# The start of a two-layer decoder trunk: x loaded over two queues ahead of everything else, matmuls of ones first, and the first norm taken from a second copy of x

## The chip, the cores and the metric

One core of one Trainium2 chip runs the whole program. The metric is device microseconds of one execution; the lower the better. The program's times below are the median of three executions, and the profile is of one more execution.

## What is computed

The reference is a trunk of two layers (DEPTH = 2) on 512 tokens of width 1024, all in float32. Only the start of a layer matters here:

```python
for i in range(DEPTH):
    h = rmsnorm(x, norm_g[i])
    z = h @ w_in[i]
    (a_q, a_k, ..., i_q, i_k, i_w, ..., merge) = jnp.split(z, offsets, axis=-1)
    ...
def rmsnorm(x, g):
    xf = x.astype(jnp.float32)
    y = xf * lax.rsqrt(jnp.mean(xf * xf, axis=-1, keepdims=True) + EPS)
    return (y * g.astype(jnp.float32)).astype(x.dtype)
```

After the projection each layer runs three attention mixers, three gated up-projections, an output projection and a gated per-layer embedding. A last rmsnorm gives the output. Rotary angles come from `positions`: cos and sin of position times eight frequencies.

## The kernel before

**Layout.** The residual x lies transposed, features on partitions: eight tiles `X` of 128 features by 512 tokens (KT = 8). A projection gives 128 output features by 512 tokens in one PSUM bank. The row factor of the norm (one over the root mean square of a token) is not applied to x but to the products afterwards, so products can start before it is known. The gain `norm_g` is applied to x at once, from the first eight columns (`ng`) of a table of small parameters called `small` (505 columns).

**Three matmuls for one.** Every operand is split into a high part, rounded to the fp32r format that TensorE takes in one pass, and the remainder: `HI` and `LO` for x (`scaled_split`, ACT and DVE), `whi` and `wlo` for weights (`weights`, ACT or POOL for the first, DVE or POOL for the second). A product of 128 features is HI by whi, LO by whi and HI by wlo for each of eight feature tiles: 24 matmuls of 512 columns (`product`). Weights come in pieces of 128 by 512 (`raw`, four buffers) by DMAs that SP issues, two pieces to a product.

**The start of layer 0.** The first unit of weights (`IKBK`) and the eight `X` tiles are loaded on SP. ACT issues the loads of the positions (`posi`), the frequencies (`inv`), `small` and the constants (`consts`: identity and masks). Then come three products of 24 matmuls each (IKBK, IQ0, IQ1) and the token products (`tok_product`): 4 pairs of weight tiles, tokens on the PSUM partitions, 352 columns, 96 matmuls. In between, `statistics` squares the eight `X` tiles on ACT (`square`), adds them up on DVE or POOL, sums over the partitions with 16 one-column matmuls against `ones` (`rms_stats`; each is float32 and runs as two instructions, so eight calls), forms the factor with an integer guess and three Newton steps of small DVE instructions (`rsqrt`), and spreads it over a tile `R` with one float32 matmul. `angles` makes cos and sin: some 20 DVE instructions on 128 by 32 elements in a row, each reading the one before, with the two Sin activations on ACT at the end. `rope_tables` transposes cos and sin on TensorE and multiplies them by `R`; every product of queries and keys needs the result.

**What sets the order.** Nothing is issued as written. Each call is recorded in a `Plan`; `Plan.put_down` (L387) then walks a list schedule: an operation has a cost per engine (`Plan.cost`, L336) and a rank, its place in the program plus `plan.shift`; each engine takes what could start first, with a small price for a late rank. The result is a fixed order of instructions on each engine, written out at L468, which is why all rows of the profile carry that line. Engines then run in this order, each waiting for its inputs. A DMA is issued by an engine's own instruction stream (SP's or ACT's), in its place in that order.

**Completion counters of DMAs.** Under the plan, the tile framework gives each DMA one of eight completion counters in turn (`DMAHW0` to `DMAHW7`). A DMA that takes a counter waits, at its issue, until the DMA that had this counter before it has landed, whichever queue that one is on. In the built program this stands as a wait on the issuing instruction.

Of the kernel before, what the change touches and what calls it, by code (L numbers as in the profile page):

```python
# [15 lines left out]
AF = mybir.ActivationFunctionType  # L16
ALU = mybir.AluOpType
# [4 lines left out]
EPS = 1e-6  # L22
# [10 lines left out]
NWS = 4  # L33
NKB = 10
URGE = 0.002
THETA = 500000.0

SPLITS = (
# [180 lines left out]
class Plan:  # L219
# [116 lines left out]
    def cost(self, engine, op):  # L336

        if op.call == "dma_start":
            return 0.65, 2.4
        n = max(x.columns() for x in op.ins + op.outs)  # L340
        psum = any(x.tile.space == "psum" for x in op.ins + op.outs)
        if engine == "tensor":
# [44 lines left out]
    def put_down(self):  # L387
        names = ("tensor", "vector", "scalar", "gpsimd", "sync")
        free = dict.fromkeys(names, 0.0)
        port = 0.0  # L390
        held = {(e, o.seq): self.shares(e, o) for o in self.ops for e in o.engines}

        def begin(e, op):
# [30 lines left out]
        while done < len(self.ops):  # L424
            best = None
            for e in names:
                pick = None
                for op in can[e]:
                    at = begin(e, op)
                    key = at + (0.0 if e == "tensor" else URGE) * op.rank  # L430
                    if pick is not None and (pick[2], pick[1].rank) < (key, op.rank):
                        continue
                    if len(op.engines) > 1 and e != min(op.engines, key=lambda x: finish(x, op)):
                        continue
                    pick = (at, op, key)
                if pick and (best is None or pick[0] < best[0]):
                    best = (pick[0], e, pick[1])
            if best is None:
                raise RuntimeError("the plan is stuck")
            at, e, op = best  # L440
            us, lag = (op.us, op.lag) if e == op.engines[0] else self.cost(e, op)
            op.engine, op.start = e, at
            free[e] = at + us
            if held[e, op.seq]:
                port = at + us
            for x in op.engines:
                can[x].remove(op)
            done += 1
            end = at + us + lag
            for o in op.next:  # L450
                o.ready = max(o.ready, at + us if o.engines == (e,) and op.call != "dma_start" else end)
                o.left -= 1
                enter(o)
            for t in op.tiles.values():
                t.uses -= 1
                t.end = max(t.end, end)
                if t.uses == 0 and t.space != "dram":
                    slots[t.ring].append((t.end, t.slot))
                    give(t.ring)
# [9 lines left out]


@with_exitstack
def trunk_kernel(ctx, tc, xT, pT, pos, freq, W, WK, small, con, out):
    nc = tc.nc
    plan = Plan(tc)
    V, G, A, T, SY = [plan.engine(e) for e in ("vector", "gpsimd", "scalar", "tensor", "sync")]
# [44 lines left out]
        return t.bitcast(F32)  # L520

    posi = const("posi", [P, NQ], I32)
    A.dma_start(posi, pos)
    inv = const("inv", [P, 8], F32)
    A.dma_start(inv, freq)
    consts = const("consts", [P, NCO], F32)
    ident = consts[:, CO["ident"][0] : CO["ident"][1]]
    mask = consts[:, CO["mask"][0] : CO["mask"][1]]
# [1 line left out]
    valid = consts[:, CO["valid"][0] : CO["valid"][1]]  # L530
    ones = const("ones", [P, P], F32)
    V.memset(ones, 1.0)


    def rsqrt(y, v, n, off=False):
# [27 lines left out]

    def rms_stats(sums):

        pst = tr_ps()
        for b in range(NQ):
            c = slice(b * P, (b + 1) * P)
            T.matmul(pst[:, b : b + 1], sums["acc"][:, c], ones[:, 0:1], start=True, stop=False)
            T.matmul(pst[:, b : b + 1], sums["last"][:, c], ones[:, 0:1], start=False, stop=True)  # L570
        ms = sb("ms", (P, NQ), bufs=2)
        V.tensor_scalar(ms, pst[:, 0:NQ], 1.0 / D, EPS, ALU.mult, ALU.add)
        rstd = sb("rstd", (P, NQ), bufs=2)
        rsqrt(rstd, ms, NQ)
        prb = tr_ps()
# [10 lines left out]
        SY.dma_start(raw[:, : src.shape[1]], src)  # L586
        return raw

    def weights(src, n):

        his, los = [], []
        step = S // n * n
        for c in range(0, src.shape[1], step):
            w = min(step, src.shape[1] - c)
            raw = load_raw(src[:, c : c + w])
            hi = sb("whi", (P, S), F32R, pool=wp, bufs=NWS)
            lo = sb("wlo", (P, S), F32R, pool=wp, bufs=NWS)
            AG.copy(hi[:, :w], raw[:, :w])
# [10 lines left out]
    sin8 = const("sin8", [P, NQ, 8], F32)  # L609
    cos8 = const("cos8", [P, NQ, 8], F32)  # L610
    nsin8 = const("nsin8", [P, NQ, 8], F32)
    A.activation(sin8[:, 0, 0:1], ones[:, 0:1], AF.Sin)

    def angles():

        V.tensor_copy(posf, posi)
# [40 lines left out]
    sums = {}  # L657
    for l in range(L):
        sm = plan.tile(lp, (P, NSM), F32, nm("small"), "small", 1)
        A.dma_start(sm, small[l])  # L660

        def par(name, a=0, n=None):
            s0, s1 = SM[name]
# [3 lines left out]


        if l == 0:
            have["w"] = weights(W[l, UNIT["IKBK", 0]], P)  # L670
            xs = []
            for d in range(KT):
                t = sb("X", pool=bp)
                SY.dma_start(t, xT[:, d, :])
                xs.append(t)
            A.dma_start(consts, con)
            resid = [xT[:, d, :] for d in range(KT)]
        else:
            resid = []
# [15 lines left out]
            return his, los  # L695

        HI, LO = scaled_split(xs, "ng")
        if l == 0:
            angles()


        def tok_product(pieces, n, evac, banks):
# [13 lines left out]

        def statistics():
            if l == 0:
                for t in xs:
                    square(sums, t)  # L720
            rstd, R, _ = rms_stats(sums)
            if l == 0:
                Cr, Sr = rope_tables(R)
# [657 lines left out]
def _arrange(x, p, positions, norm_g, w_in, diff_lambda, diff_subln_g,  # L1381
# [56 lines left out]
    for i in range(NQ):  # L1438
# [3 lines left out]
        con[:, CO["valid"][0] + i] = (t[:, 0] >= 31).astype(np.float32)  # L1442
    return {
        "xT": np.ascontiguousarray(x[0].T.reshape(KT, P, S).transpose(1, 0, 2)),
        "pT": np.ascontiguousarray(p[:, 0].transpose(0, 2, 1).reshape(L, 2, P, S).transpose(0, 2, 1, 3)),
        "pos": np.ascontiguousarray(positions[0].reshape(NQ, P).T),
        "freq": freq,
# [17 lines left out]
```

## Time and profile before

| | us |
|---|---|
| time, median of 3 (1420.03 to 1420.48) | 1420.24 |
| the profiled execution's own time | 1421.58 |
| its span, first to last instruction | 1419.8 |
| TensorE matmuls busy, share of the span | 1380.1 (97%) |
| DVE, ACT, POOL busy | 1050.4, 784.6, 586.2 |
| mean granted TensorE clock | 0.992 |
| moved by DMA | 115.5 MB read, 4.7 MB written |

The busy time of TensorE says that it has something in flight nearly always; idle stretches are at the start, around 30 to 62 us, and in the last 25 us. The granted clock is given as a share of full speed; 1.00 is 2.4 GHz and 0.50 is 1.2 GHz.

### The profile page before, as it was taken

Reading aid. Unit: us, or ns where it says so; the run is one execution under the profiler, and the core shown is the slowest. Engines: PE = TensorE matmul, PEld = TensorE weight load, DVE = VectorE, ACT = ScalarE, POOL = GpSimd, SP = SyncE. Lnnn points to the kernel's source line nnn. Section 1 sums busy time; section 2 is a strip of 40 time slices with the busy share of each in tenths; the row PEclk is TensorE's granted clock in tenths of the full one; section 3 lists DMA queues with packets and bytes.
Section 4 is the critical chain, followed back from the end, with each engine's and each line's share of the span. In section 5 each row is a group of like instructions: output and inputs, shape, how many; then the busy total and the mean of one; then the engine's idle time right before and its main releaser. Section 6 shows DMA issues by size and latency. Waiting matters only on the chain.

```text
span 1419.8 us, 20706 instructions
## 1 busy us (share of the span) xinstructions
PE 1380.1 (97%) x6842; PEld 1151.0 (81%) x6842; DVE 1050.4 (74%) x2346; ACT 784.6 (55%) x1820; POOL 586.2 (41%) x623
## 2 busy tenths in 40 slices
PE   7899999999999999999999999999999999999995
PEld 5788887888888888888888888878888888888884
DVE  7768888878887566556885888888888855656664
ACT  4556666766764456324444666666676644643431
POOL 3646468544453152121452744873455323313120
PEclk9999999999999999999999999999999999999997
DMA  5222322111222221343422232312112222124321
GB/s 171 92 74 81 105 88 67 60 61 60 68 74 82 83 89 60 107 145 102 142 80 98 82 97 62 95 59 69 60 60 75 67 89 85 61 83 156 94 81 60
DMA packets 67069, 121.56 MB, mean 86 GB/s; under 512 B 7696, under 2 KB 10000, under 8 KB 66960
## 3 DMA queue, kind: packets, MB, share of 16 engines
q1 hardware_dynamic: 61632, 110.91, 24.7%
q10 hardware_dynamic: 5328, 9.31, 1.9%
q8 instruction: 54, 0.88, 0.2%
q14 instruction: 55, 0.45, 0.1%
HBM read 115.48 MB, written 4.72 MB: 85 GB/s over the span
## 4 chain that ended last, share of the span: by engine, by line
PE 87%; POOL 3%; DVE 3%; issue 2%; ACT 1%; DVEq 0%; POOLq 0%; ACTq 0%
PE mm L468 69%; PE at L468 19%; POOL nt L468 1%; DVE t L468 1%; POOL Q L468 1%; POOL t L468 1%; POOL wlo L468 1%; DVE BV L468 0%; ACT t L468 0%; POOL whi L468 0%; ACT o L468 0%; DVE pc L468 0%; DVE wlo L468 0%; POOL K L468 0%; ACT P L468 0%
## 5 line engine op out<-in xcount | busy, mean ns | idle before, releaser
L468 PE MATMUL mm<-HI,whi 128*128 128x512 f32 x1232 | 496.5, 404 | 10.2 <-ACT HI L468 9.3
L468 PE MATMUL mm<-HI,wlo 128*128 128x512 f32 x1232 | 486.1, 395 | 0.3
L468 PE MATMUL mm<-LO,whi 128*128 128x512 f32 x1232 | 484.9, 394 | 0.0
L468 POOL TENSOR_SCALAR whi<-raw 128x512 fp32r<-128x512 f32 (+1 forms) x188 | 128.5, 685 | 530.7 <-PE mm L468 381.5
L468 POOL TENSOR_TENSOR wlo<-raw,whi 128x512 fp32r<-128x512 f32 (+1 forms) x198 | 268.8, 1361 | 176.7 <-ACT whi L468 160.3
L468 PEld LDWEIGHTS mm<-HI,whi 128*128 128x128 f32 x1232 | 232.5, 189 | 49.2 <-ACT HI L468 9.3
L468 PEld LDWEIGHTS mm<-HI,wlo 128*128 128x128 f32 x1232 | 231.7, 188 | 49.9 <-DVE wlo L468 1.1
L468 ACT CAST whi<-raw 128x512 fp32r<-128x512 f32 (+1 forms) x208 | 126.9, 612 | 255.6 <-PE mm L468 194.4
L468 PEld LDWEIGHTS mm<-LO,whi 128*128 128x128 f32 x1232 | 232.5, 189 | 39.3 <-issue 0.7
L468 DVE TENSOR_TENSOR wlo<-raw,whi 128x512 fp32r<-128x512 f32 (+1 forms) x198 | 146.2, 742 | 81.2 <-ACT whi L468 44.5
L468 ACT ACTIVATE P<-P,mx 128x512 f32<-128x512 f32 (+3 forms) x256 | 142.4, 557 | 67.9 <-DVE mx L468 67.2
L468 PE MATMUL at<-K,Q 128*128 128x256 f32 (+3 forms) x608 | 139.0, 325 | 1.4 <-DVE VW L468 1.1
L468 PEld LDWEIGHTS at<-K,Q 128*128 128x128 f32 x608 | 104.1, 189 | 19.3 <-ACT VS L468 1.4
L468 DVE TENSOR_TENSOR t<-mm,R 128x512 f32<-128x512 f32 x100 | 68.9, 689 | 59.5 <-PE mm L468 56.7
L468 DVE CUSTOM_DVE_ANT_0 P<-at,consts 128x128 f32<-128x128 f32 x208 | 93.4, 469 | 20.4 <-PE at L468 19.6
L468 DVE TENSOR_TENSOR PTl<-at,PTh 128x512 fp32r<-128x512 f32 x192 | 87.0, 484 | 26.8 <-ACT PTh L468 20.0
L468 POOL TENSOR_TENSOR Q<-t,Q 64x512 fp32r<-64x512 f32 x64 | 87.1, 1361 | 33.9 <-ACT Q L468 27.1
L468 ACT ACTIVATE P<-P,rc 128x128 f32<-128x128 f32 x192 | 92.1, 552 | 9.5 <-DVE rc L468 8.8
L468 PE MATMUL at<-consts,P 128*128 128x128 f32 x560 | 96.1, 273 | 0.3 <-DVE P L468 0.3
L468 ACT CAST PTh<-at 128x512 fp32r<-128x512 f32 x192 | 74.2, 420 | 36.2 <-PE at L468 32.2
L468 PEld LDWEIGHTS at<-consts,P 128*128 128x128 f32 x560 | 71.8, 140 | 23.0 <-DVE P L468 1.2
L468 PE MATMUL mm<-BRh,whi 128*128 128x512 f32 x192 | 77.0, 406 | 0.0
(209 smaller groups left out, 2146.7 us busy)
## 6 DMA issues: line engine op xcount, KB each, us to landing
raw<-W SPq DMA_DIRECT2D x396, 256.0 KB, 2.6
raw<-WK SPq DMA_DIRECT2D x16, 176.0 KB, 2.2
X<-xT SPq DMA_DIRECT2D x8, 256.0 KB, 6.8
X<-xT ACTq DMA_DIRECT2D x8, 256.0 KB, 3.2
res<-X ACTq DMA_DIRECT2D x8, 256.0 KB, 2.0
X<-res ACTq DMA_DIRECT2D x8, 256.0 KB, 3.2
out<-t SPq DMA_DIRECT2D x6, 256.0 KB, 2.6
K<-pT ACTq DMA_DIRECT2D x4, 256.0 KB, 3.3
```

Source lines behind the costliest of these rows:

```text
L468: getattr(getattr(self.nc, op.engine), call)(*real, **kw)
```

## The change

Five edits. (1) `small` is loaded in two pieces, its first eight columns before all else, the rest later. (2) The eight `X` tiles are issued in turn by ACT (even) and SP (odd), four behind each piece of the first weights; `posi`, `inv`, the rest of `small`, `consts` and the first use of the Sin table come behind them on ACT. (3) Nine float32 matmuls of `ones` by `ones`, 128 by 128 each, stand ahead of the first product and write a spare bank. (4) In layer 0 the sum of squares of a token comes from `xN`, x with tokens on partitions: four loads of 128 by 1024 (512 KB each) on SP, and one Square activation with `accum_out` for each; the eight squares, their additions and the one-column matmuls go, in layer 0 alone. `angles` is called behind these. (5) The planner's cost of a DMA: 0.5 us on the issuing engine instead of 0.65, landing 1.4 us later instead of 2.4, plus 0.1 us and bytes at 370 GB/s on one shared wire.

```diff
@@ Plan.cost
         if op.call == "dma_start":
-            return 0.65, 2.4
+            return 0.5, 1.4
@@ Plan.put_down
+            if op.call == "dma_start":
+                tile = (op.outs + op.ins)[0]
+                end = wire = max(end, wire) + 0.1 + tile.shape[0] * tile.columns() * 4 / 370000.0
@@ trunk_kernel
     posi = const("posi", [P, NQ], I32)
-    A.dma_start(posi, pos)
     inv = const("inv", [P, 8], F32)
-    A.dma_start(inv, freq)
...
     V.memset(ones, 1.0)
+    spare = at_ps()
+    for _ in range(WARM):
+        T.matmul(spare[:, :P], ones, ones, start=True, stop=True)
...
     def rms_stats(sums):
-        pst = tr_ps()
-        for b in range(NQ):
-            c = slice(b * P, (b + 1) * P)
-            T.matmul(pst[:, b : b + 1], sums["acc"][:, c], ones[:, 0:1], start=True, stop=False)
-            T.matmul(pst[:, b : b + 1], sums["last"][:, c], ones[:, 0:1], start=False, stop=True)
+        if "rows" in sums:
+            total = sums["rows"]
+        else:
+            total = tr_ps()[:, 0:NQ]
+            for b in range(NQ):
+                c = slice(b * P, (b + 1) * P)
+                T.matmul(total[:, b : b + 1], sums["acc"][:, c], ones[:, 0:1], start=True, stop=False)
+                T.matmul(total[:, b : b + 1], sums["last"][:, c], ones[:, 0:1], start=False, stop=True)
         ms = sb("ms", (P, NQ), bufs=2)
-        V.tensor_scalar(ms, pst[:, 0:NQ], 1.0 / D, EPS, ALU.mult, ALU.add)
+        V.tensor_scalar(ms, total, 1.0 / D, EPS, ALU.mult, ALU.add)
...
-    def weights(src, n):
+    def weights(src, n, between=()):
...
             raw = load_raw(src[:, c : c + w])
+            for fetch in between[c // step :][:1]:
+                fetch()
...
-    A.activation(sin8[:, 0, 0:1], ones[:, 0:1], AF.Sin)
...
-        A.dma_start(sm, small[l])
+        if l == 0:
+            A.dma_start(sm[:, 0:KT], small[l, :, 0:KT])
+        else:
+            A.dma_start(sm, small[l])
...
         if l == 0:
-            have["w"] = weights(W[l, UNIT["IKBK", 0]], P)
-            xs = []
-            for d in range(KT):
-                t = sb("X", pool=bp)
-                SY.dma_start(t, xT[:, d, :])
-                xs.append(t)
+            xs = [sb("X", pool=bp) for _ in range(KT)]
+
+            def fetch(*tiles):
+                for d in tiles:
+                    (SY if d % 2 else A).dma_start(xs[d], xT[:, d, :])
+
+            have["w"] = weights(W[l, UNIT["IKBK", 0]], P, (lambda: fetch(0, 1, 2, 3), lambda: fetch(4, 5, 6, 7)))
+            A.dma_start(posi, pos)
+            A.dma_start(inv, freq)
+            A.dma_start(sm[:, KT:], small[l, :, KT:])
             A.dma_start(consts, con)
+            A.activation(sin8[:, 0, 0:1], ones[:, 0:1], AF.Sin)
...
-        if l == 0:
-            angles()
...
         def statistics():
             if l == 0:
-                for t in xs:
-                    square(sums, t)
+                sums["rows"] = sb("ss", (P, NQ), bufs=2)
+                for b in range(NQ):
+                    plan.shift = 70 * (b // 2)
+                    t = sb("P", (P, 1280), bufs=3)[:, :D]
+                    SY.dma_start(t, xN[b])
+                    A.activation(t, t, AF.Square, accum_out=sums["rows"][:, b : b + 1])
+                plan.shift = 0
+                angles()
```

**ACT's start.** What stands first on ACT before, with the waits of each instruction (the number behind a name tells buffers apart; DVE, Pool and Activation are the counters of those engines):

```order
L468 DMA posi_77<-pos 128x4
L468 DMA inv_89<-freq 128x8
L468 ACT_TABLE_LOAD
L468 ACTIVATE sin_8_93<-ones_79 128x1 [waits DVE_49]
L468 DMA small_97<-small 128x505
L468 DMA consts_101<-con 128x772 [waits DMAHW0_49]
L468 CAST whi_105<-raw_81 128x512 [waits DMAHW1_49]
L468 CAST whi_111<-raw_91 128x512 [waits DMAHW3_49]
L468 ACTIVATE t_117<-X_95 128x512 [waits DMAHW4_49]
L468 ACTIVATE HI_123<-X_95,small_97 128x512 [waits DMAHW6_49]
```

And on ACT in the changed kernel:

```order
L472 DMA small_79<-small 128x8
L472 DMA X_87<-xT 128x512
L472 DMA X_95<-xT 128x512
L472 DMA X_109<-xT 128x512
L472 DMA X_115<-xT 128x512 [waits DMAHW0_49]
L472 DMA posi_121<-pos 128x4 [waits DMAHW2_49]
L472 DMA inv_125<-freq 128x8 [waits DMAHW4_49]
L472 DMA small_79<-small 128x497 [waits DMAHW5_49]
L472 DMA consts_134<-con 128x772 [waits DMAHW7_49]
L472 ACT_TABLE_LOAD
L472 ACTIVATE sin_9_138<-ones_77 128x1 [waits DVE_49]
L472 ACTIVATE HI_142<-X_87,small_79 128x512
```

Nine DMA issues instead of four now stand ahead of the first `HI`, five of them with a wait for an earlier DMA; the one of `consts` waits for counter 7, which was last taken by `raw_107`.

**SP's start.** SP in the changed kernel (before, it issued raw, raw, the eight X in a row, then four raw):

```order
L472 DMA raw_81<-W 128x512
L472 DMA X_89<-xT 128x512
L472 DMA X_97<-xT 128x512
L472 DMA raw_107<-W 128x512
L472 DMA X_113<-xT 128x512 [waits DMAHW1_49]
L472 DMA X_119<-xT 128x512 [waits DMAHW3_49]
L472 DMA raw_127<-W 128x512 [waits DMAHW6_49]
L472 DMA raw_130<-W 128x512 [waits DMAHW0_49]
L472 DMA P_136<-xN 128x1024 [waits DMAHW1_49]
L472 DMA P_140<-xN 128x1024 [waits DMAHW2_49]
L472 DMA P_144<-xN 128x1024 [waits DMAHW3_49]
L472 DMA raw_152<-W 128x512 [waits DMAHW4_49,DVE_49]
```

`raw_107` is SP's fourth load, and three of the four loads of `xN` now stand ahead of the weights of the third product (`raw_152`).

**TensorE in the third product.** The transposes of cos and sin (`at_301`, `at_329`) stood behind the one-column matmuls and among the token products before; now they stand in the third product (`mm_297`):

```order
L472 MATMUL mm_211<-HI_194,wlo_228 128x512
L472 MATMUL mm_297<-HI_142,whi_290 128x512
L472 MATMUL at_301<-consts_134,t_83 128x128 x4
L472 MATMUL mm_297<-LO_148,whi_290 128x512
L472 MATMUL mm_297<-HI_142,wlo_295 128x512
L472 MATMUL mm_297<-HI_146,whi_290 128x512
L472 MATMUL mm_297<-LO_156,whi_290 128x512
L472 MATMUL mm_297<-HI_146,wlo_295 128x512
L472 MATMUL mm_297<-HI_154,whi_290 128x512
L472 MATMUL at_329<-consts_134,t_91 128x128 x4
```

`t_83` holds cos, which needs all of `angles` before it, and 23 matmuls of the third product stand behind its transposes.

## Rows read from the trace of the kernel before

**Rows 1.** The page, part 1: busy us, share of the span, instructions of TensorE.
```profile
PE 1380.1 (97%) x6842; PEld 1151.0 (81%) x6842; DVE 1050.4 (74%) x2346; ACT 784.6 (55%) x1820; POOL 586.2 (41%) x623
```
**Rows 2.** Waits of TensorE, 0 to 60 us: us in total, times, longest.
```profile
PE mm L468 <- ACT HI L468: 9.3, 1, 9.3
PE mm L468 <- ACT whi L468: 1.5, 1, 1.5
PE mm L468 <- DVE t L468: 1.1, 1, 1.1
```
**Rows 3.** Timeline of TensorE, first product: start us, us, engine, line, operation.
```profile
11.12 0.63 PE L468 MATMUL mm<-HI,whi 128*128 128x512 f32 x1
11.55 0.63 PE L468 MATMUL mm<-LO,whi 128*128 128x512 f32 x1
...
12.73 0.40 PE L468 MATMUL mm<-LO,whi 128*128 128x512 f32 x1
...
12.97 0.40 PE L468 MATMUL mm<-HI,wlo 128*128 128x512 f32 x1
```
**Rows 4.** Timeline of ACT, 0 to 5 us; idle time and releaser in brackets.
```profile
1.64 1.28 ACT L468 ACT_TABLE_LOAD   x1 [1.64 <-PEq L1457]
...
3.62 0.33 ACTq L468 DMA_DIRECT2D consts<-con  x1
4.00 1.14 ACT L468 CAST whi<-raw 128x512 fp32r<-128x512 f32 x2 [0.86 <-DMA posi<-pos]
```
**Rows 5.** SP's third and fourth load: issue in the timeline; KB and us to landing.
```profile
1.63 0.90 SPq L468 DMA_DIRECT2D X<-xT  x2
...
X<-xT SPq DMA_DIRECT2D x2, 256.0 KB, 6.5
```
**Rows 6.** Windows: us, busy (x) per engine, clock, DMA share, GB/s.
```profile
2.00:6.00 4.00, 0.00 (x0) 0.00 (x0) 1.52 (x4) 2.26 (x4) 0.00 (x0) 1.00 0.86 248
6.00:14.00 8.00, 4.69 (x13) 3.45 (x14) 4.88 (x11) 5.41 (x9) 0.00 (x0) 1.00 1.00 373
```
**Rows 7.** Groups by form, 0 to 30 us, ACT, DVE, POOL: xcount, busy us, mean ns.
```profile
L468 ACT ACTIVATE HI<-X,small 128x512 fp32r<-128x512 f32 x8 | 5.3, 718 | 0.6 <-DMA X<-xT 0.6
L468 ACT ACTIVATE t<-X 128x512 f32<-128x512 f32 x8 | 4.5, 620 | 2.9 <-DMA X<-xT 2.9
...
L468 DVE SCALAR_TENSOR_TENSOR LO<-X,small,HI 128x512 fp32r<-128x512 f32 x8 | 5.9, 791 | 3.0 <-ACT HI L468 3.0
...
L468 POOL TENSOR_TENSOR wlo<-raw,whi 128x512 fp32r<-128x512 f32 x3 | 4.2, 1413 | 0.2
L468 POOL TENSOR_TENSOR wlo<-raw,whi 128x352 fp32r<-128x352 f32 x3 | 3.1, 1042 | 2.0 <-ACT whi L468 1.9
```
**Rows 8.** Timeline of DVE and ACT, the chain of `angles`.
```profile
15.55 5.97 DVE L468 SCALAR_TENSOR_TENSOR ang<-kk,ang 128x32 f32<-128x32 f32 x8
...
22.20 0.65 DVE L468 SCALAR_TENSOR_TENSOR ang<-kk,ang 128x32 f32<-128x32 f32 x3
...
24.61 0.23 ACT L468 ACTIVATE cos<-kk 128x32 f32<-128x32 f32 x1 [1.28 <-DVE kk L468]
```
**Rows 9.** Timeline of TensorE at the one-column matmuls and the transposes behind them.
```profile
30.41 0.38 PE L468 MATMUL at<-ones,g 128*128 128x1 f32 x2 [0.59 <-DVE g L468]
...
32.22 0.64 PE L468 MATMUL at<-consts,t 128*128 128x128 f32 x4
```
**Rows 10.** Windows, as rows 6: right behind rows 9, and near the end of the program.
```profile
32.60:36.20 3.60, 3.60 (x17) 3.60 (x16) 3.19 (x20) 0.59 (x1) 0.00 (x0) 0.57 0.39 123
1402.00:1403.00 1.00, 1.00 (x6) 1.00 (x6) 0.00 (x0) 0.00 (x0) 0.00 (x0) 0.50 0.00 0
```
**Rows 11.** Timeline of TensorE at 1401.68 us: idle time in brackets.
```profile
1401.68 0.47 PE L468 MATMUL at<-ones,t 128*128 128x1 f32 x2 [3.78 <-ACT t L468]
```
**Rows 12.** Timeline of ACT and TensorE: `R`, and the first weights behind the token products.
```profile
37.39 0.58 ACT L468 COPY R<-at 128x512 f32<-128x512 f32 x1 [3.91 <-PE at L468]
...
48.55 0.50 PE L468 MATMUL mm<-whi,HI 128*128 128x512 f32 x1 [1.54 <-ACT whi L468]
```

More of the change, by code (lines that the diff above doesn't have):

```diff
@@ L35 @@
 URGE = 0.002
+WARM = 9
 THETA = 500000.0
@@ L389, in put_down @@
         free = dict.fromkeys(names, 0.0)
-        port = 0.0
+        port = wire = 0.0
         held = {(e, o.seq): self.shares(e, o) for o in self.ops for e in o.engines}
@@ L471, in trunk_kernel @@
 @with_exitstack
-def trunk_kernel(ctx, tc, xT, pT, pos, freq, W, WK, small, con, out):
+def trunk_kernel(ctx, tc, xT, xN, pT, pos, freq, W, WK, small, con, out):
     nc = tc.nc
@@ L1444, in _arrange @@
         "xT": np.ascontiguousarray(x[0].T.reshape(KT, P, S).transpose(1, 0, 2)),
+        "xN": np.ascontiguousarray(x[0].reshape(NQ, P, D)),
         "pT": np.ascontiguousarray(p[:, 0].transpose(0, 2, 1).reshape(L, 2, P, S).transpose(0, 2, 1, 3)),
```

## The prediction

> **What bounds the kernel now.** Read the page first: TensorE's matmuls are busy 97% of the span [rows 1], so nearly all of the 1419.8 us is TensorE's own work, which the change leaves alone but for a few instructions. What can be won or lost is time in which TensorE stands still or runs slowly, and the change touches only the first 50 us or so. So read next who TensorE waits for there, then the stretch as a timeline. TensorE's first matmul waits 9.3 us for the first `HI` [rows 2]. The first eight matmuls then start 0.43 us apart, later ones 0.23 to 0.24 [rows 3]: 512 columns at 1.2 and at 2.4 GHz. (The clock column says 1.00 in this stretch [rows 6]; here the spacing is the better witness.) At 30.41 us comes a wait of 0.59 us and then 1.8 us of one-column matmuls, up to the transposes at 32.22 [rows 9]; right behind them the granted clock is 0.57 for 3.6 us [rows 10]. Then there are waits of 1.1 and 1.5 us [rows 2], the last ending at 48.55 us, at the first weights behind the token products [rows 12].
>
> I count what TensorE loses up to that matmul. 9.3 for the start; 8 x 0.2 = 1.6 at half clock; 0.6 + 1.8 = 2.4 for the statistics; (1 - 0.57) x 3.6 = 1.5 for the clock behind them; 1.1 + 1.5 = 2.6. Sum 17.4. Useful until then: 72 matmuls of 512 columns at 0.23, 68 token matmuls at 352/512 of that, 0.16, eight transposes at 0.64/4 = 0.16 [rows 9] and about 1 us for the matmul of `R`: 29.7. As 48.55 - 29.7 = 18.9, another 1.5 goes in waits too small to list.
>
> **When the first product starts.** This decides most. ACT issues nine DMAs ahead of its first `HI`, and the last, `consts`, waits for the landing of `raw_107`, SP's fourth load. That such a wait holds the instructions behind it is shown before: the issue of `consts` at 3.62 us waited for `posi`, and the copy `whi` behind it began only at 4.00, with that DMA as the releaser [rows 4]. SP's third and fourth loads before were issued at 1.63 and 2.1 us and landed 6.5 us later [rows 5]; so I take 8.6 us for `raw_107`, the row that is nearest. Bounds: seven loads of 262 KB share the way; all at the later rate of 373 GB/s from 2 us on gives 6.9 us; at the early 248 GB/s up to 6 us, and in equal shares with what ACT has put behind, 9.5 us [rows 6]. Then on ACT the issue 0.33, the table load 1.28 [rows 4], a short Sin 0.23 [rows 8] and the first `HI` 0.72 [rows 7]: 2.6 us. First matmul at 11.2 us (9.5 to 12.1): 1.9 us later than before, not earlier.
>
> **The matmuls of ones.** Nine, each between 0.16 us (a transpose of 128 columns, one instruction at full clock [rows 9]) and four times that, 0.64 (two instructions at half clock), from about 1 us on: done between 2.5 and 6.8 us. They cost nothing, since TensorE idles until 11.2 anyway; were that cover gone and the first `HI` there at 5 us, they would cost up to 1.8. What they are for is likely lost: in this trace an idle time of 3.78 us [rows 11] was followed by a clock of 0.50 [rows 10], and here at least 4.4 us lie between them and the first product.
>
> **The first product** is paced by DVE: eight `LO` of 0.79 and one `wlo` of about 0.7 make 7.0 us [rows 7] against 24 x 0.23 = 5.5 of matmuls. It loses 1.5; a half clock start hides in this but for some 0.3. I take 1.8 (1.5 to 2.2).
>
> **The transposes in the third product.** TensorE reaches `at_301` after 49 matmuls: 11.2 + 11.3 + 1.8 = 24.3 us. It needs cos in `t_83`. DVE, from 11.2 on: eight `LO` and three `wlo`, 8.4 us, then some 30 instructions of 0.22, since three took 0.65 [rows 8], 6.6 us, and 0.3 for ACT's cos: 26.5 us with DVE undisturbed. But before, eight such instructions took 5.97 us instead of 1.8 [rows 8], while POOL ran `wlo` instructions of 1.41 and 1.04 us [rows 7]. In the changed order three of POOL's (1.4 + 1.0 + 1.0 = 3.4) can fall into this stretch: 29.9 us. Between ends so alike in kind I take half, 28.2: TensorE stands for 3.9 us (2.2 to 5.6). That is about the idle time that ended at half clock [rows 10, 11]; eight slow matmuls would cost 1.6 [rows 3]; I count half, 0.8.
>
> **The statistics.** Gone are the 2.4 us and the 1.5 us of low clock behind them. The four Squares of 1024 columns are about 1.24 us each (twice 0.62 [rows 7]), beside TensorE's work; but the last two stand behind cos on ACT, with a table load, a `whi`, a copy and a DMA issue between: 5.5 us from cos, so 32.9. Behind that on DVE two shuffles and some sixteen short instructions, 5 us: 37.9. TensorE gets to the matmul of `R` at 28.2 + 1.3 + 5.3 + 3.4 + 0.8 = 39.0, so it does not wait for it (0 to 1.5; I take 0.3). `R` is there 2.6 us later than before [rows 12]. The table load for Exp and what DVE waits for from it now lie ahead of `R`, which shortens the way from `R` to 48.55 from 11.2 to about 9.8 us: 49.8. TensorE, with 59 token matmuls in between (9.4 us), is there at 49.4 and waits 0.4.
>
> **The loads of xN.** 2.1 MB more, 5.6 us at 373 GB/s. Queued behind three of them is `raw_152`: 5.6 MB from 2 us on, by the two rates, land by 18.5 us; `whi` and `wlo` 2 us more. TensorE wants them at 24, so 3.5 us of cover hide them; without it each of the three would cost 1.4. The fourth waits for the first Square and is in by 24, ahead of ACT's 31.
>
> **The planner's costs** reorder neighbours in the rest of the program, with the same work on each engine; I count 0, and 1 us to either side.
>
> **Sum.** 11.2 + 1.8 + 3.9 + 0.8 + 0.3 + 0.4 = 18.4 against 18.9: TensorE is 0.5 us ahead in work (12 more token matmuls are done), while the first matmul behind them comes 1.2 us later. What follows hangs on both in turn, so I take the middle, +0.3 us. Against the profiled execution that is 1421.6 + 0.3 = 1421.9; the median of the runs lies 1.3 lower, so **1420.5 us**: no change that could be measured (0.2%, 2.8 us, is about what a measurement of this kernel can tell).
>
> **Rivals.**
>
> *Early release, faster.* `raw_107` lands at 6.9 us and POOL's `wlo` miss the chain of `angles`: first matmul 9.5, stall 2.2, no fall of the clock. 1.7 + 1.7 + 0.8 = 4.2 us better: 1416.3. For it: the small loads `posi` and `inv` no longer stand in the early stretch that ran at 248 GB/s. Against it: in that stretch both queues already had loads outstanding, so a second queue alone is no cure. The Trainium skill, "DMA: Bandwidth & Descriptors", section "Issuing engines are not separate DMA queues", says that loads issued by different engines run on the same sixteen DMA engines and that spreading them saves only the time of issuing; by it x lands no sooner for being on two queues, and the sum stands. Chance 0.24.
>
> *The queue doesn't hold ACT at all*, and the first `HI` follows its own tile, at about 4.6 us: first matmul near 6, another 3.5 us off: 1412.8. Rows 4 speak against it. Chance 0.04.
>
> *A late cos, slower.* `raw_107` at 9.5 and all three of POOL's `wlo` in the way: first matmul 12.1, `t_83` at 30.8, a stall over 5 us and half clock for sure behind it. 0.9 + 1.7 + 0.8 = 3.4 us, 1423.9. It decides from the point where the stall passes 3.8 us. For it: on DVE before, most of this chain was lost to POOL. Chance 0.29.
>
> *The ones hold the clock* through 4.4 idle us or more. Then the start is at full speed, but DVE paces the product: 0.3 us, inside the forecast.
>
> **Numbers.** Forecast, within 0.2%: 0.43, its own range 1417.6 to 1422.9. Faster 0.24 + 0.04 = 0.28, slower 0.29. The range for 8 in 10, with the ends of both rivals and the 1 us of the planner: 1415.5 to 1425.0.
>
> **What would show it.** In the profile after: the first `HI` behind a table load that follows the issue of `consts`, with `raw_107` landing just before; first matmul at 11 us, spaced 0.43; the second stall of TensorE at the transposes of cos, of 2 to 6 us, released by DVE; no one-column matmuls and no clock of 0.5 near 33 us; then a first matmul on later weights near 50 us. The prediction is wrong if the first `HI` starts before 8 us, or if TensorE doesn't stop at the transposes.

## The result, and the profile after

The changed kernel takes **1430.32 us** (median of 4 runs, 1428.42 to 1433.41) against 1420.36 us (4 runs, 1420.03 to 1421.41): a ratio of 1.0072, 95% interval 1.006 to 1.0085. It is 10 us slower. The forecast was 1420.5 us, range 1415.5 to 1425.0, so the time lies outside it. The profiled execution took 1433.41 us, the longest of the four.

The page's first part, against [rows 1]: TensorE, DVE, ACT and POOL have nearly the same work in a span that is 11.8 us longer.

```profile
span 1431.6 us, 20707 instructions
...
PE 1385.0 (97%) x6844; PEld 1153.3 (81%) x6844; DVE 1055.0 (74%) x2347; ACT 781.4 (55%) x1815; POOL 575.9 (40%) x621
```

**The start came out much as forecast.** ACT's timeline, to set against [rows 4]: the issue of `consts` is held until 8.44 us, the table load behind it has `raw` (SP's fourth load) as its releaser, and the first `HI` begins at 10.21 us, although the first X tile had landed at 5.3 us.

```profile
8.44 0.33 ACTq L472 DMA_DIRECT2D consts<-con  x1
8.80 1.28 ACT L472 ACT_TABLE_LOAD   x1 [8.80 <-DMA raw<-W]
10.10 0.20 ACT L472 ACTIVATE sin<-ones 128x1 f32<-128x1 f32 x1
10.21 5.00 ACT L472 ACTIVATE HI<-X,small 128x512 fp32r<-128x512 f32 x8
```

TensorE's timeline, against [rows 3, 9]: first matmul at 11.05 us; the next two follow after 0.70 and 0.59 us, then they start 0.43 us apart until 14.05, at a granted clock of 0.50; a wait of 3.15 us at the transposes of cos and sin, and again 0.43 us behind it; 1.28 us at the matmul of `R`. The windows below it are to be read as [rows 10]: the granted clock is 0.50 behind the wait at 27.19 us, and once more in layer 2. (From here on the two layers are called 1 and 2; layer 1 is what the sections ahead call layer 0.)

```profile
11.05 0.77 PE L472 MATMUL mm<-HI,whi 128*128 128x512 f32 x1 [6.39 <-ACT HI L472]
...
13.62 0.63 PE L472 MATMUL mm<-HI,wlo 128*128 128x512 f32 x1
14.05 0.45 PE L472 MATMUL mm<-HI,whi 128*128 128x512 f32 x1
14.33 0.39 PE L472 MATMUL mm<-LO,whi 128*128 128x512 f32 x1
...
27.19 0.66 PE L472 MATMUL at<-consts,t 128*128 128x128 f32 x4 [3.15 <-DVE t L472]
...
28.43 0.63 PE L472 MATMUL mm<-HI,whi 128*128 128x512 f32 x1
28.86 0.63 PE L472 MATMUL mm<-LO,whi 128*128 128x512 f32 x1
...
39.78 1.13 PE L472 MATMUL at<-t,ones 128*128 128x512 f32 x2 [1.28 <-DVE t L472]
```
```profile
27.80:31.20 3.40, 3.40 (x12) 2.71 (x11) 1.07 (x4) 2.98 (x5) 0.00 (x0) 0.50 0.12 37
939.30:942.50 3.20, 3.20 (x9) 2.43 (x9) 3.10 (x10) 1.76 (x3) 2.76 (x6) 0.50 0.00 1
```

**Most of the loss lies far behind the start**, where no edit touched the computation. Who TensorE waits for between 60 and 1370 us, in the kernel before (us in total, times, longest):

```profile
PE at L468 <- ACT o L468: 3.7, 8, 0.5
PE at L468 <- ACT t L468: 1.1, 1, 1.1
PE mm L468 <- DVE VW L468: 1.0, 1, 1.0
PE mm L468 <- POOL whi L468: 0.9, 2, 0.5
```

and in the changed kernel, where waits for DVE's `t`, `wlo`, `gate` and `hr` are new. Two of these rows still belong to the start: the wait for POOL's `whi` ends at 59.80 us and that for `gate` at 63.87.

```profile
PE at L472 <- ACT o L472: 4.0, 8, 0.6
PE at L472 <- DVE t L472: 3.2, 2, 1.6
PE mm L472 <- DVE wlo L472: 1.6, 2, 1.0
PE at L472 <- POOL whi L472: 1.4, 1, 1.4
...
PE mm L472 <- DVE gate L472: 1.1, 1, 1.1
PE mm L472 <- DVE hr L472: 0.9, 2, 0.4
```

To see where time is lost, each instruction of DVE, ACT and POOL is paired with the one of the same name in the kernel before (counted from the end, since the tail is the same work), and the difference of their starts is taken; its median over 20 us is the **lag**. In us, for the profiled execution of the changed kernel and of six runs that follow:

| at us | changed | e1 | e2 | e10 | e4 | e11 | e12 |
|---|---|---|---|---|---|---|---|
| 100 | 3.1 | 2.2 | -2.3 | 0.7 | -6.8 | -6.6 | -6.5 |
| 180 | 4.1 | 2.3 | -0.4 | 0.9 | -5.0 | -6.5 | -4.0 |
| 300 | 6.8 | 2.3 | 3.3 | 0.9 | -0.8 | -6.4 | -6.6 |
| 760 | 7.4 | 2.8 | 3.5 | 1.4 | -0.1 | -6.0 | -6.2 |
| 1000 | 12.2 | 3.1 | 6.6 | 1.8 | 3.3 | -4.7 | -7.9 |
| 1400 | 12.0 | 2.9 | 5.7 | 1.7 | 3.3 | -5.0 | -8.0 |

The changed kernel's lag grows in two places: 100 to 300 us and 760 to 1000 us, which are the attention mixers of layer 1 and of layer 2. Layer 2 does not use the copy of x, nor the loads or matmuls that were moved. What those two places share is the order in which the plan put their instructions. Compared instruction by instruction, the two programs differ behind 130 us only in what the plan decides: nearly all differences lie between 140 and 400 us and between 820 and 1070 us, on TensorE, DVE, ACT and POOL; the loads on SP stand in the same order.

### The profile page after: what moved, and what is told of

It is laid out like the page before. It is cut to its first block, busy times and chain, and to the rows that moved or that the text cites. A ratio compares the mean times of both kernels' runs of the same rounds, so it can differ in the third digit from the quotient of the medians.

```text
span 1431.6 us, 20707 instructions
## 1 busy us (share of the span) xinstructions
PE 1385.0 (97%) x6844; PEld 1153.3 (81%) x6844; DVE 1055.0 (74%) x2347; ACT 781.4 (55%) x1815; POOL 575.9 (40%) x621
## 4 chain that ended last, share of the span: by engine, by line
PE 88%; DVE 5%; ACT 1%; POOL 1%; issue 0%; DVEq 0%; POOLq 0%; ACTq 0%
PE mm L472 69%; PE at L472 19%; DVE t L472 2%; DVE P L472 0%; POOL nt L472 0%; DVE cm L472 0%; ACT o L472 0%; ACT t L472 0%; DVE g L472 0%; DVE wlo L472 0%; DVE K L472 0%; DVE x L472 0%; DVE hr L472 0%; DVE BV L472 0%; DVE X L472 0%
## 5 line engine op out<-in xcount | busy, mean ns | idle before, releaser
L472 POOL TENSOR_SCALAR whi<-raw 128x512 fp32r<-128x512 f32 (+1 forms) x193 | 131.4, 682 | 550.7 <-PE mm L472 392.5
L472 POOL TENSOR_TENSOR wlo<-raw,whi 128x512 fp32r<-128x512 f32 (+1 forms) x194 | 260.9, 1349 | 175.6 <-ACT whi L472 148.3
L472 ACT CAST whi<-raw 128x512 fp32r<-128x512 f32 (+1 forms) x203 | 123.8, 613 | 260.5 <-PE mm L472 194.6
```

The lines of the kernel that those rows point to most:

```text
L472: getattr(getattr(self.nc, op.engine), call)(*real, **kw)
```

## Experiments

Each time is a median; the ratio is to the kernel before on the same chip, with its 95% interval. Theory A: the planner's new DMA costs (edit 5) reorder the attention parts. Theory B: the late start alone. Theory D: the list schedule's order is arbitrary. A2, named from the second set on, joins A and D: the plan falls into one of a few orders, and the cost of the order adds to that of the start.

### Edit 5 taken back (e1), and alone (e2)

```diff
-            return 0.5, 1.4
+            return 0.65, 2.4
...
-            if op.call == "dma_start":
-                tile = (op.outs + op.ins)[0]
-                end = wire = max(end, wire) + 0.1 + tile.shape[0] * tile.columns() * 4 / 370000.0
```

> The changed kernel with the planner's old DMA costs (0.65 us, landing 2.4 us later, no shared wire); edits 1 to 4 stay. Theory A (the new costs swap neighbours in the attention parts of both layers, and this loses some 7 of the 10 us): 1422 to 1424 us, the first at<-K,Q still near 52.6 us as in the changed kernel (50.3 before), and no further lag behind it. Theory B (the late start alone, everything behind it merely shifted or knocked on): 1429 to 1431 us. Theory D (the order that a list schedule falls into is arbitrary; any small change of costs moves it by several us to either side): any value from 1418 to 1432, not tied to edit 5.

Measured: 1423.55 us, ratio 1.0018 (1.0009 to 1.0027).

e2 makes the reverse edit in the kernel before, and no other.

> The kernel before with edit 5 alone (a DMA costs the planner 0.5 us, lands 1.4 us later, plus bytes on one shared wire). Theory A: 1426 to 1428 us, with the lag coming in between 60 and 240 us and again between 855 and 945 us. Theory B: 1420 to 1421 us. Theory D: any value from 1418 to 1432.

Measured: 1429.36 us, ratio 1.005 (1.0037 to 1.0062). Theory B falls with both: without edit 5 the changed kernel loses 2.5 us, and edit 5 alone loses 7. In the lag table e1 stays flat behind the start, and e2 starts ahead of the kernel before, then loses 5.6 us between 100 and 300 and 3.1 between 760 and 1000. Behind some 130 us, e1's program has the order of the kernel before on every engine, and e2's that of the changed kernel.

### The new costs at the start alone (e10)

```diff
-            return 0.5, 1.4
+            return (0.5, 1.4) if op.seq < 1000 else (0.65, 2.4)
...
-            if op.call == "dma_start":
+            if op.call == "dma_start" and op.seq < 1000:
```

> The changed kernel with the new DMA costs (and the wire) for the first 1000 recorded calls alone, the old ones for all that follow; ACT still issues the late loads. Behind some 130 us its instructions stand in the order of the kernel before. Theory A2 (start and order add up): the lag of the changed kernel near 100 us, 3.1 us, and what old costs lose later, 0.8 us: 1423 to 1425 us. Rival (the late start itself is what disturbs the attention parts): still 1428 us or more.

Measured: 1424.15 us, ratio 1.0021 (1.0012 to 1.003). The start is planned as in the changed kernel; only the order behind it is that of before, and 1.0072 falls to 1.0021: **7.2 us of the 10 are the order behind the start, 3 us the start.** (The two intervals leave some 2 us to either side.) By the traces the orders of the two programs differ nowhere ahead of 140 us. TensorE's waits from 196 to 256 us in this run are two; the kernel before has the same two there and one of 0.2 us more:

```profile
PE at L472 <- ACT o L472: 0.9, 2, 0.5
PE mm L472 <- POOL whi L472: 0.5, 1, 0.5
```

### Half of edit 5 (e7)

```diff
-            return 0.65, 2.4
+            return 0.5, 1.4
```

> The kernel before with half of edit 5: a DMA costs the planner 0.5 us and lands 1.4 us later, no shared wire. Behind the start this gives a third order of instructions, neither that of before nor that of the changed kernel. Theory A2 (a few discrete orders, each with a time of its own, none better for the costs being truer): anything from 1418 to 1432 us, and its lag against before appears only in the stretches 130 to 260 and 840 to 960 us. Theory A1 (costs that land DMAs too early make TensorE wait for weights everywhere): a lag that grows evenly along the span, 1425 to 1430 us.

Measured: 1418.36 us, ratio 0.9978 (0.9969 to 0.9987): faster than before, where the whole edit lost 7 us. Its lag goes from +0.5 us at 100 to -1.5 at 300 and -4.4 at 1000, in the stretches that were expected, and another 1.6 us come near the end (its profiled execution, 1415.68 us, was the fastest of ten). So truer or cheaper costs of a DMA are not slow in themselves; what counts is which order they tip the plan into. The other half, the wire alone, was not run.

### Why the changed kernel's order is slow (e13 to e16)

In layer 1 TensorE waits here in the changed kernel (its timeline, then DVE's):

```profile
242.13 0.39 PE L472 MATMUL mm<-HI,wlo 128*128 128x512 f32 x1
244.10 1.10 PE L472 MATMUL at<-KCb,t 128*128 128x64 f32 x8 [1.58 <-DVE t L472]
```
```profile
241.13 1.09 DVE L472 TENSOR_TENSOR cm<-cm,gate 128x8 f32<-128x8 f32 x1
242.14 0.68 DVE L472 MAX8 m<-acc 128x8 f32<-128x512 f32 x1
242.75 0.69 DVE L472 TENSOR_TENSOR cm<-cm,consts 128x8 f32<-128x8 f32 x1
243.37 0.68 DVE L472 TENSOR_TENSOR t<-mm,R 128x512 f32<-128x512 f32 x1
```

The kernel before at the same place, DVE and then TensorE: the two short `cm` instructions take 0.27 and 0.17 us, `t` waits for TensorE and not the other way round.

```profile
231.98 0.27 DVE L468 TENSOR_TENSOR cm<-cm,gate 128x8 f32<-128x8 f32 x1
232.28 0.17 DVE L468 TENSOR_TENSOR cm<-cm,consts 128x8 f32<-128x8 f32 x1
...
234.11 0.69 DVE L468 TENSOR_TENSOR t<-mm,R 128x512 f32<-128x512 f32 x1 [0.32 <-PE mm L468]
```
```profile
235.04 0.39 PE L468 MATMUL mm<-HI,wlo 128*128 128x512 f32 x1
235.27 1.00 PE L468 MATMUL at<-KCb,t 128*128 128x64 f32 x8
```

e13 moves these matmuls nine matmuls later, in both layers, and nothing else:

```diff
+        for a, b in ((1875, 1986), (7410, 7521)):
+            for k in range(4):
+                self.ops[a + k].start = self.ops[b].start + 0.001 * (k + 1)
```

> The changed kernel with one group of matmuls moved on TensorE alone, in each layer: the four at<-KCb,t that stood directly behind the product whose result t they need (the wait of 1.58 us at 244.10 us and again at 937.62 us) stand nine matmuls of the next product later. All other engines keep the changed kernel's order. If these waits carry a part of the order's 7 us: 1.6 us less in each layer, 3.2 us, and 1.6 us more where the half clock behind the wait (939.2 to 942.6 us in the profile) goes with it: 1425.5 to 1427.1 us. Rival (DVE is late as a whole, so the next matmul that needs it waits instead): 1429 to 1431 us.

Measured: 1430.45 us, ratio 1.007 (1.0057 to 1.0084): no gain. The wait went to the next instruction that needs DVE:

```profile
248.28 0.33 PE L475 MATMUL at<-consts,P 128*128 128x128 f32 x1 [1.46 <-DVE P L475]
```

So the delay is in DVE's stream there and not at that one matmul. Windows between the same two marks of the program (from DVE's `o<-at,sub,g` to the first matmul on `BRh`; what the plan puts between them is not quite the same, 176 instructions on DVE against 174) give DVE 74.09 us in the changed kernel and 69.60 before, in 84.5 and 82.1 us (columns as in [rows 6]: TensorE, its weight loads, DVE, ACT, POOL):

```profile
176.10:260.60 84.50, 79.87 (x429) 66.25 (x428) 74.09 (x176) 52.16 (x141) 55.65 (x74) 1.00 0.23 75
```
```profile
172.00:254.10 82.10, 79.95 (x434) 66.92 (x432) 69.60 (x174) 52.74 (x144) 57.59 (x70) 1.00 0.24 78
```

e14 to e16 give work back by a table of places in the program, with the starts of the plan kept (cut; e15 has the 25 entries that concern DVE, e16 adds the edit of e13):

```diff
+        moved = {
+            'scalar': [1040, 1079, 1596, 1822, 1953, ...],
+            'gpsimd': [1147, 1149, 1202, 1718, 2026, 2030, ...],
+            'vector': [1870, 2230, 2288, 2291, 2733, ...],
+        }
+        for engine, seqs in moved.items():
+            for k in seqs:
+                self.ops[k].engine = engine
```

> The changed kernel, its plan's order kept, but 43 instructions behind the first 1000 calls (whi, wlo and t, which more than one engine may do) written to the engine that the plan of before gave them. In the stretch from the second o of layer 1 to BRh the changed kernel has DVE busy 83.6 us against 78.4 before: two more wlo, longer short instructions beside POOL. Theory C (DVE's load in the attention parts is the 7 us): 1423 to 1426 us. Rival (the order on each engine is, whichever engine has the work): 1428 to 1432 us.

> As the run before it, but only the 25 of these instructions that move from or to DVE (wlo and t); whi stays where the changed kernel has it. Theory C: the same gain, 1423 to 1426 us. If the engine of whi counts (it feeds wlo): in between, 1426 to 1429 us. Rival (order): 1428 to 1432 us.

> All 43 instructions on the engines of before, and the four at<-KCb,t nine matmuls later, which alone gained nothing since DVE's P came late next. Theory C: with DVE relieved that wait should now pay: 1 to 3 us below the run with the engines alone. Rival: the same as that run, within 1 us.

Measured: 1437.44 us, ratio 1.0114 (1.0097 to 1.013); 1436.08 us, 1.0107 (1.0092 to 1.0122); 1439.98 us, 1.0131 (1.0116 to 1.0146). All are slower than the changed kernel, and than every range that had been given. Theory C's gain did not come. The same piece of the program in e14:

```profile
176.30:259.80 83.50, 79.63 (x429) 66.14 (x428) 69.16 (x172) 52.44 (x142) 56.90 (x73) 1.00 0.24 75
```

DVE is back at the load of before, 69.16 us, and the piece is 1.0 us shorter than in the changed kernel. But the run loses more elsewhere: its lag is 8.4 us at 300 and 16.4 at 1000, against 6.8 and 12.2. Moving work also puts instructions into new places on the engines that take them over, so these runs show that DVE's share of the work is not what costs the 7 us by itself; they do not show that DVE's lateness has no part in it.

What the traces do show is where the time of an order goes: into idle time of TensorE in the two attention stretches. The idle times that the timeline gives ahead of its matmuls, summed over 100 to 320 and 780 to 1070 us of each profiled execution, go by the order and hardly by the start; e2, e4 and the changed kernel lie 10 us apart at 100 us:

| order behind the start | runs | TensorE idle, us |
|---|---|---|
| third | e7, e12 | 5.0, 5.4 |
| of before | before, e1, e10, e11 | 6.1, 6.1, 6.1, 6.7 |
| changed | changed, e9, e2, e4 | 11.5, 11.3, 12.3, 12.7 |
| changed, engines of before | e14, e15 | 17.4, 16.0 |

That is some 5 to 6 us for the changed order; the half clock behind one of these waits is another 1.7 (3.4 us at 0.50, in layer 2 of the changed kernel and in layer 1 of e2 and e9). Which property of an order makes these waits long stays open.

### What holds the start: the queue of ACT (e4, e5)

e4 gives the late loads to SP; e5 does so with the old costs.

```diff
-            A.dma_start(posi, pos)
-            A.dma_start(inv, freq)
-            A.dma_start(sm[:, KT:], small[l, :, KT:])
-            A.dma_start(consts, con)
+            SY.dma_start(posi, pos)
+            SY.dma_start(inv, freq)
+            SY.dma_start(sm[:, KT:], small[l, :, KT:])
+            SY.dma_start(consts, con)
```

> The changed kernel with posi, inv, the rest of small and consts issued by SP instead of ACT, so that the completion counter of raw_107 holds SP and not ACT. All theories: the first HI behind its own X tile near 4.5 us and the first matmul at 5 to 7 us. Theory B (the late start costs the 10 us): 1420 to 1424 us. Theory A: 1425 to 1428 us, since the lag in the two attention parts stays. SP is held until 8.4 us, so the third and fourth weights can come late; a stall of up to 3 us in the second product would show it.

> The changed kernel with both repairs: the planner's old DMA costs, and posi, inv, the rest of small and consts issued by SP. Theory A2 (the plan falls into one of a few orders behind the start; the old costs bring back that of before, and the start and the order add up): late loads on SP were 5.7 us faster under the new costs, so 1423.6 - 5.7 = 1417.9, and down to 1415 us if the start keeps all of the 8.6 us that it led by near 100 us in that run. Theory B2 (what the start gains is lost again in the next wait, whatever the order): 1420 to 1423 us.

Measured: e4 1424.64 us, ratio 1.0029 (1.0018 to 1.0041), against 1.0072 with ACT held; e5 1418.89 us, 0.9981 (0.9972 to 0.999), against e1's 1.0018. Releasing ACT wins 6 us under the new costs and 5 under the old (and 7 between e10 and e11, below, where the order behind the start is that of before). ACT's timeline in e4: the first `HI` begins at 6.29 us instead of 10.21, and its X tile is there.

```profile
4.38 1.28 ACT L472 ACT_TABLE_LOAD   x1 [4.38 <-DMA small<-small]
5.67 0.20 ACT L472 ACTIVATE sin<-ones 128x1 f32<-128x1 f32 x1
5.78 0.60 ACT L472 CAST whi<-raw 128x512 fp32r<-128x512 f32 x1
6.29 3.21 ACT L472 ACTIVATE HI<-X,small 128x512 fp32r<-128x512 f32 x5
```

In the changed kernel all eight `HI` ran without a wait for X, from 10.21 us on; what they stood behind was an issue that waited. The first matmul comes at 7.06 us, just past the 5 to 7 expected; the stall feared in the second product is a wait of 0.99 us for `wlo`, at 16.22 us. e5's time is 1 us above what A2 gave.

### The ones (e3, e9)

e3 sets `WARM = 0`. e9 plans the nine matmuls and does not write them, so that the order of all else stays:

```diff
+                if op.seq in self.dropped:
+                    continue
```

> The changed kernel without the matmuls of ones (WARM = 0). They ran from 1.03 to 4.66 us, TensorE idled until 11.05 us and the first product ran at half clock. Theories A and B: 1430 us, within 1 us, the first product as before at 11 us and 0.43 us apart. Theory D: off by several us, since without the ones the planner sees another time for TensorE at the start.

> The changed kernel with the nine matmuls of ones planned as before but not written out, so that the order of all else is the changed kernel's (leaving them out of the plan as well gave 1436.4 us and another order). The prediction's term (they cost nothing and keep no clock): within 1 us of the changed kernel, 1429 to 1432 us. Rival (they do something for the clock of the first product): 2 to 5 us slower.

Measured: e3 1436.36 us, ratio 1.0109 (1.0094 to 1.0124); e9 1429.86 us, 1.0059 (1.0047 to 1.0072). With the order held the ones are worth nothing that can be measured. Leaving them out of the plan as well is 5 to 7 us slower than the changed kernel and e9, though no matmul of the computation was touched; A and B had both given 1430 us. By its lag e3 is 1.5 us ahead of the kernel before at 100 us, 6.4 behind at 300 and 13.7 at 1000, again in the two attention stretches: it is the purest case of theory D here.

### The statistics of xN (e6, e8)

e6 undoes edit 4 in e1, e8 undoes it in e5:

```diff
-                sums["rows"] = sb("ss", (P, NQ), bufs=2)
-                for b in range(NQ):
...
-                angles()
+                for t in xs:
+                    square(sums, t)
```

> The changed kernel with the planner's old costs and without edit 4: the row statistics and angles as before, no loads of xN. Prediction's terms (statistics cost TensorE 2.4 us and 1.5 us of low clock, ACT's late release 1.9 us): against old costs with xN, 1423.6 us, the 3.9 us come back, and 1 to 3 us of stalls behind the statistics of xN go: 1425 to 1427 us. Rival (the statistics are hidden either way): 1422 to 1424 us. Rival (loads of xN are what holds the start back, by keeping the weights out): under 1421 us.

> As the run with both repairs (old costs, late loads on SP), but the statistics as before, without xN. If xN pays once ACT is released: 2 to 4 us slower than that run (2.4 us of one-column matmuls and 1.5 us of low clock come back). If its 2.1 MB keep the weights of the second and third product out (1.6 and 1.0 us of waits for wlo were seen with late loads on SP): 1 to 3 us faster than that run.

Measured: e6 1424.05 us, ratio 1.0019 (1.001 to 1.0028), level with e1's 1.0018; e8 1421.82 us, 1.0002 (0.9993 to 1.0011), against e5's 0.9981. With ACT held the statistics of xN are worth nothing (the rival's time, not the 3.9 us of the prediction's terms); with ACT free they win 3 us. Behind some 120 us e6 and e8 follow the order of before on every engine; e8 lags 1.0 us at 100 us where e5 leads by 2.8, so the difference is made at the start.

### The parts put together (e11, e12)

e11 is e10 with the late loads on SP. e12 is the changed kernel with the late loads on SP and the wire for the first 1000 calls alone (0.5 and 1.4 us throughout). Behind the start its order is e7's:

```diff
-            if op.call == "dma_start":
+            if op.call == "dma_start" and op.seq < 1000:
```

> New DMA costs for the first 1000 calls alone, and the late loads on SP. Theory A2: the start as in the run with late loads on SP and new costs (6.9 us ahead of before near 100 us), the order of before behind it, which lost 1.6 to 2.2 us of such a lead in the run with both repairs: 1415 to 1417 us. Rival (a lead of the start is eaten up by the next late weights): 1418 to 1421 us.

> As the run before it, but for calls behind the first 1000 the costs of half of edit 5 (0.5 us, 1.4 us, no wire), which bring the third order. In the kernel before with that half, this order won 2.4 us between 200 and 300 us, 2.7 us by 1000 us and 1.5 us at the end. Theory A2: 1409 to 1413 us, the fastest of all. Rival (the third order gains only from its own start): 1415 to 1417 us.

Measured: e11 1416.92 us, ratio 0.997 (0.9958 to 0.9983); e12 **1412.58 us**, 0.9936 (0.9924 to 0.9949), 9 us faster than the kernel before and 18 faster than the changed one. Both lie where A2 had them. From the changed kernel e12 differs in one condition of the planner and in the queue of four loads.

## Why the prediction was wrong

Every sign that the prediction named for itself is in the profile, and the time was wrong all the same: all of them lie in the first 50 us, and most of the loss does not.

- **First matmul, 11.2 us (9.5 to 12.1): right**, 11.05, by the path that it gave; e4 shows that the held queue is the cause.
- **The ones, nothing: right.** They ran from 1.03 to 4.66 us, the granted clock was 0.50 again from 11.0 to 14.05 us, and e9 shows no difference. The rival that they hold the clock falls.
- **First product, 1.8 us lost: right.** (The prediction reads the first eight matmuls of before as 0.43 us apart; the first two gaps there were 0.79 and 0.59 us, which changes its sum of 1.6 us by 0.2.) TensorE reached the transposes at 27.19 - 3.15 = 24.04 us, forecast 24.3; less 11.05 and 49 x 0.23 = 11.3 that leaves 1.7.
- **Stall at the transposes, 3.9 us: 3.15** in this profile, 2.3 in e9's and 1.2 in e10's, which have the same order there. Inside the bounds or below. The clock behind it was counted half, 0.8 us; here it fell in full, 3.4 us at 0.50, 1.7 us, behind less idle time than the 3.78 us of [rows 11]. In the other two it did not fall there.
- **Matmul of `R`, 0.3 us: 1.28.** The sum up to here is 11.05 + 1.7 + 3.15 + 1.7 + 1.3 = 18.9, against 18.0 forecast. The next term, 0.4 us at the first weights behind the token products, was nothing: that matmul starts at 50.86 us (forecast 49.8) without a wait. The kernel before lost 18.9 up to it by the prediction's count.
- **What the forecast left out of the start** came right behind: between 52 and 66 us TensorE waits 1.5 us for `VW`, 1.4 for POOL's `whi` and 1.1 for `gate`, 4.0 in all, against 1.7 before. In e10 the first weights come at 48.15 us, ahead of before; then it waits 1.5 and 1.4 us for the same two, and the clock is 0.50 for 3.4 us from 57.8 on. By e10 the start as a whole costs 3 us, forecast +0.3: off, but inside the range, since 1420.4 + 3 is 1423.4.
- **The statistics**: the 2.4 us of one-column matmuls are gone, but e6 against e1 shows that with ACT held nothing is won by it. There it is not the stall that takes the gain back: e1 has none at the transposes, and waits 2.1 us each for POOL's and ACT's `whi` instead. For the changed kernel itself this was not tried.
- **"The planner's costs reorder neighbours in the rest of the program, with the same work on each engine; I count 0, and 1 us to either side": this step failed.** It cost 7.2 us (e10), or 7.1 alone (e2). No row of the trace stood behind the 0. "The same work on each engine" is nearly so, and was taken for "the same time": in the attention parts TensorE waits for what DVE, POOL and ACT make, and the order decides how long. The lag table puts 3.7 us of it between 100 and 300 and 4.8 between 760 and 1000, in the slowest of the four executions; in e9, with the same order, it is 5.7 and 2.7. That a swap puts a short DVE instruction beside one of POOL's, as at 241 us, is one way in which this happens; that it makes up the 7 us is not shown.
- **Rivals.** *Late cos* named a slower time, but by a longer stall at the transposes; the stall was shorter than forecast. *Early release* was not what happened; with ACT released by an edit it is (e5). None of the rivals was the order of the rest, and none reached 1430 us.

In *Early release* the prediction weighs a rule of the Trainium skill, "DMA: Bandwidth & Descriptors", section "Issuing engines are not separate DMA queues": DMAs of different issuing engines run on the same sixteen DMA engines, and spreading them saves only the time of issuing. From it the prediction took that x lands no sooner. In the trace it does: the first tile at 5.3 us against 8.0 before, the last at 10.7 against 13.7, with these times from issue to landing, before and after:

```profile
X<-xT SPq DMA_DIRECT2D x8, 256.0 KB, 6.8
```
```profile
X<-xT SPq DMA_DIRECT2D x4, 256.0 KB, 5.3
X<-xT ACTq DMA_DIRECT2D x4, 256.0 KB, 5.7
```

But 0.64 MB of `small` and `consts`, which shared the way with x before, are issued behind it now, and no run has the one without the other, so the rule is neither borne out nor refuted here. The sum stood for another reason: ACT was held until 8.8 us and could not use the tiles that were there.

## What to carry to other kernels

Where a list schedule sets the order, every cost that it reads, and every operation that it counts, is an edit of the whole program: compare the orders far from the edit, and price the edit with the order held (here: costs that apply to the first calls only, or an operation that is planned and not written). Put no DMA issue that can wait ahead of the work of a busy engine; the wait holds everything behind it, also what has its data.

## What the runs showed of the hardware

- **Equal waits do not always end at the same clock.** Behind the wait of 1.58 us at 937.62 us the granted clock fell to 0.50 for 3.4 us; behind its twin of 1.58 us at 244.10 us it did not, and neither did it behind one of 2.30 us at 26.39 us in e9. In e2 it was the first of the two (1.61 us) that was followed by it. Its matmuls are 0.23 us apart at first and 0.43 from 241.08 us on. The changed kernel's wait, then e2's:

```profile
937.62 1.10 PE L472 MATMUL at<-KCb,t 128*128 128x64 f32 x8 [1.58 <-DVE t L472]
```
```profile
239.06 1.10 PE L471 MATMUL at<-KCb,t 128*128 128x64 f32 x8 [1.61 <-DVE t L471]
...
240.52 0.40 PE L471 MATMUL mm<-HI,wlo 128*128 128x512 f32 x1
240.75 0.53 PE L471 MATMUL mm<-HI,whi 128*128 128x512 f32 x1
241.08 0.63 PE L471 MATMUL mm<-LO,whi 128*128 128x512 f32 x1
241.51 0.63 PE L471 MATMUL mm<-HI,wlo 128*128 128x512 f32 x1
```

- **A short DVE instruction can take as long as POOL's.** `cm<-cm,gate` on 128 by 8 elements took 0.27 us before and 1.09 in the changed kernel, where it began 0.23 us after a `wlo` of POOL and ended with it; the next one, `cm<-cm,consts`, 0.69 us instead of 0.17, ended with POOL's second `wlo`, at 243.42 us:

```profile
240.90 2.52 POOL L472 TENSOR_TENSOR wlo<-raw,whi 128x512 fp32r<-128x512 f32 x2
```

The Trainium skill, "SBUF — State Buffer", section "SBUF: two separate sides", says that DVE and GpSimd share one pair of ports, and that a DVE instruction with two inputs in SBUF and a GpSimd instruction that reads SBUF exclude each other there: whichever starts first holds the pair for its whole instruction. Both `cm` instructions have two inputs in SBUF, `wlo` reads `raw` and `whi` there, and each `cm` ended with a `wlo` (242.22 us and 242.19, 243.44 and 243.42), so the trace agrees. Which short instruction stands beside a `wlo` is decided by the order.
